# Inverses of the recurrent heads: row steps on blocks of 32 with a block product, or on blocks of 16 with two correction steps on TensorE

## The chip, the cores and the metric

The kernel runs on one core of a Trainium2 chip. The metric is the device time of one execution in microseconds. TensorE (PE in the profile) multiplies matrices and writes to PSUM, VectorE (DVE), ScalarE (ACT) and GpSimd (POOL) do elementwise work, and SyncE (SP) issues most DMA transfers. Each engine runs its own instructions in the order in which they were built, and waits on semaphores for the others.

## The reference, cut to what matters

One layer of a hybrid decoder for a prompt of 256 tokens and 8 single decode tokens: a half-step SwiGLU feed-forward network (FFN), then a mixing stage with 16 attention heads beside 16 recurrent heads (RWKV-7) of size 64, then a second FFN. Everything is float32. The recurrent part of the prompt is this scan:

```python
def step(S, inp):
    r_t, lw_t, k_t, v_t, kk_t, a_t = inp
    sa = jnp.einsum('bhij,bhj->bhi', S, -kk_t)
    S = (S * jnp.exp(lw_t)[:, :, None, :] + sa[..., None] * (kk_t * a_t)[:, :, None, :]
         + v_t[..., None] * k_t[:, :, None, :])
    return S, jnp.einsum('bhij,bhj->bhi', S, r_t)
```

The kernel works on it in chunks of 64 tokens. Inside a chunk the terms `sa` depend on each other through a strictly triangular 64x64 matrix G of products of the scaled kk and b vectors, so each head and chunk needs the inverse of (I - G): 16 heads x 4 chunks = 64 inverses.

## The kernel before, in words

The token columns are T = 264 (256 + 8). `first_ffn` streams weights through `gemm`: a tile of 128x512 float32 is loaded by SP (`raw`, six buffers), split by ACT into a rounded part (`hi`, L122) and by DVE, or POOL for one chunk in four of the mixing stage, into the rest (`lo`, L57), and three products per 128 rows accumulate in a PSUM bank `acc`. `mixing` does the same with the 38 column tiles of w_in (`win`), then w_out in three passes, and `second_ffn` follows.

The work between the weight products is made of Python generators. `spawn` puts one in a list, and `tick`, called after each chunk of four weight blocks in `win` and in w_out, advances each by one `yield`. `pause(n)` skips n ticks. So `yield` and the constants DWAIT, PW and NSTEP decide how the small work is interleaved in the program. A scheduler then reorders instructions within each engine's queue by its own model of time and priorities; what it makes of a program can be read from the built instruction lists.

The pairs of heads p = 0 to 7 are grouped in four batches of n = 2. For each pair `prep` forms decays, normalised keys and the score matrices: `gm` (L423) is the masked 128x512 tile of one half h for four chunks, whose left 64 columns hold G in the rows of the same half. `gm` is stored to DRAM (`scr`, named sa in the profile), L426. When a batch's pairs are done (`bt.left`), `chain` goes on:

- X and Y are loaded from `scr` as one row of partitions for each 32x32 diagonal block, in four copies (ng = 4) that share the columns of the work (L475, L476; tiles X and Xt).
- 30 steps, each a multiplication into `st` and an addition into Y on DVE (L486, L487), invert the 32x32 blocks.
- Y goes to DRAM (`scr2`, named sb, L491) and comes back as `TT` with tokens on partitions (L496). DWAIT ticks are left for each of the two trips.
- The identity is added (L503), the upper left block transposed by DVE (TN, L506), and two rounds of sixteen 32x32 products (L513, L524), each followed by an ACT copy (zs, TT), fill the off-diagonal block.
- TT multiplies KR (`wus`, L538), and products with W, uv and gm, three state steps S, the group norm and the output gate follow.

`dec_rwkv` updates the decode states in 16 slices on DVE and POOL (tiles ld, t, sa, yr), and `attend` handles two heads of attention: scores (L73 m<-s,q), softmax on DVE and ACT, three transposes a head (L730 to L732), and products with V. All of this runs among the w_in products. Before the first pass of w_out, `need` drains what that pass depends on; `drain` ticks all tasks, the other chains and the attention among them. The program's three passes of w_out take pairs 0 to 5, the attention, and pairs 6 and 7.

`early(pi)` issues DMAs on ACT's queue, held in program order, during the first FFN.

Of the kernel before, what the change touches and what calls it, by code (L numbers as in the profile page):

```python
# [7 lines left out]
F32 = mybir.dt.float32  # L8
F32R = mybir.dt.float32r
AF = mybir.ActivationFunctionType  # L10
ALU = mybir.AluOpType
AX = mybir.AxisListType

P = 128
# [10 lines left out]
HALF = (slice(0, 64), slice(64, 128))  # L25
PARTS = [8, 7, 7, 7, 7, 7]
BATCH = [2, 2, 2, 2]
# [2 lines left out]
NS, NH, NT, NLD = 53, 40, 27, 6  # L30
NGM, NKR, NUV, NTT = 10, 5, 3, 2
NSTEP = 4
DWAIT = (8, 8, 8, 4)
LOP = (8,)
PW = (2, 1, 3, 2, 2)
ALPHA = math.exp(-0.5)
# [10 lines left out]
def body(tc, I, O):  # L47
    nc = tc.nc
    V, A, G, TE, SP = nc.vector, nc.scalar, nc.gpsimd, nc.tensor, nc.sync
# [6 lines left out]
    def tt(e, out, a, b, op):  # L56
        return e.tensor_tensor(out=out, in0=a, in1=b, op=op)  # L57

    def stt(out, a, s, b, op0, op1):
        return V.scalar_tensor_tensor(out=out, in0=a, scalar=s, in1=b, op0=op0, op1=op1)  # L60

    def ts(e, out, a, s1, op0, s2=None, op1=None):
        k = {} if op1 is None else dict(op1=op1)
        e.tensor_scalar(out=out, in0=a, scalar1=s1, scalar2=s2, op0=op0, **k)  # L64
# [4 lines left out]
    def bc(ap, shape):  # L69
        return ap.broadcast_to(list(shape))  # L70

    def mm(out, lhsT, rhs, start=True, stop=True, **k):
        TE.matmul(out, lhsT, rhs, start=start, stop=stop, **k)  # L73
# [16 lines left out]
    def pause(n):  # L90
        for _ in range(n):
            yield

    with ExitStack() as ctx:
# [4 lines left out]
        dp = ctx.enter_context(tc.tile_pool(name="dp", bufs=1, space=bass.MemoryType.DRAM))  # L99
# [5 lines left out]
        def tmp(shape=(P, T), dt=F32):  # L105
            pool, n = cur[0]
            return pool.tile(list(shape), dt, tag="t", bufs=n, name=uid("t"))
# [4 lines left out]
        def mp():  # L112
            return pp.tile([P, 512], F32, tag="m", bufs=NM, name=uid("m"))
# [41 lines left out]
        class Norm:  # L155
# [11 lines left out]
            def square(self, x, e=0, pin=False):  # L167
                sq = slot()
                keep = tc.keep_in_program_order if pin else lambda i: i
                if e:  # L170
                    keep(tt(V, sq, x, x, ALU.mult))
                else:
                    keep(act(sq, x, AF.Square))
                self.sums[e].append(sq)
                if len(self.sums[e]) == 3:
                    a, b, c = self.sums[e]
                    keep(tt((G, V)[e], b, b, a, ALU.add))
                    self.sums[e] = [b, c]
# [10 lines left out]
        def early(pi):  # L189
            keep = tc.keep_in_program_order  # L190
            if pi == 1:
                keep(A.dma_start(C, I["cst"]))
                keep(A.dma_start(ss, I["shs"]))
            elif pi in (2, 3):
                nm, ck = (("ks", "ck"), ("vs", "cv"))[pi - 2]
                keep(A.dma_start(O[nm][:, 0:127, :], I[ck][:, 1:128, :]))
# [93 lines left out]
        def mixing_body(mx, n2, n3):  # L290
# [3 lines left out]
            def ring(shape, tag, bufs):  # L294
                return mx.tile(list(shape), F32, tag=tag, bufs=bufs, name=uid(tag))
# [6 lines left out]
            ident, bo, cm = C[:, CID:CID + P], C[:, CBO:CBO + P], C[:, CCM:CCM + P]  # L302
# [12 lines left out]
            sa = fix((P, 64), "sa")  # L315
            yd = fix((P, 64), "yd")
            nbat = len(BATCH)
            scr = [dp.tile([BATCH[b] * 16, 1024], F32, tag=f"sa{b}", name=f"sa{b}") for b in range(nbat)]
            scr2 = [dp.tile([BATCH[b] * 16, 1024], F32, tag=f"sb{b}", name=f"sb{b}") for b in range(nbat)]
            mixed = [None] * 16  # L320
            have = [False]

# [28 lines left out]
            def prep(p, bt, k, xrr, xk, xv):  # L351
# [7 lines left out]
                sg, a = tmp(), tmp()  # L359
# [56 lines left out]
                for h in range(2):  # L416
                    r = HALF[h]
                    gp = mp()
                    for c in range(4):
                        mm(gp[:, c * P:(c + 1) * P], BK[r, c, :, :], KR[r, 0:2, c, :])  # L420
                    gm = ring((P, 4, P), "gm", NGM)
                    bt.Gm[k][h] = gm
                    tt(V, gm, gp.rearrange("p (c t) -> p c t", c=4), bc(msk.unsqueeze(1), (P, 4, P)), ALU.mult)  # L423
                    for blk in range(2):
                        x = blk * 32
                        SP.dma_start(  # L426
                            scr[bt.i].rearrange("(h b k c) (s t) -> h b k s c t", h=2, b=2, c=4, s=32)[h, blk, k],
                            gm[h * 64 + x:h * 64 + x + 32, :, x:x + 32])
                    yield
                kp = mp()  # L430
                for tb in range(2):
# [31 lines left out]
            def chain(bt):  # L463
                n = bt.n
                while bt.left:
                    yield
                nr = n * 16
                ng = P // nr
                if ng == 3:
                    ng = 2  # L470
                nj = 32 // ng
                X = ring((ng * nr, 32, 32), "X", 1)
                Y = ring((ng * nr, nj, 32), "Xt", 1)
                for g in range(ng):
                    SP.dma_start(X[g * nr:(g + 1) * nr], scr[bt.i].rearrange("r (s t) -> r s t", s=32))  # L475
                    SP.dma_start(Y[g * nr:(g + 1) * nr],  # L476
                                 scr[bt.i].rearrange("r (j g t) -> g r j t", g=ng, t=32)[g])
                TT = ring((P, n * 4, 64), "TT", NTT)
                for h in range(2):
                    G.memset(TT[h * 64 + 32:h * 64 + 64, :, 0:32], 0.0)  # L480
                yield from pause(DWAIT[bt.i])
                for s in range(1, 31):
                    m, w = -(-s // ng), 31 - s
                    t = ring((ng * nr, m, w), "st", 2)
                    shp = (ng * nr, m, w)
                    tt(V, t, bc(X[:, s:s + 1, s + 1:], shp), bc(Y[:, :m, s:s + 1], shp), ALU.mult)  # L486
                    tt(V, Y[:, :m, s + 1:], Y[:, :m, s + 1:], t, ALU.add)  # L487
                    if s % NSTEP == 0:
                        yield
                for g in range(ng):  # L490
                    SP.dma_start(scr2[bt.i].rearrange("r (j g t) -> g r j t", g=ng, t=32)[g], Y[g * nr:(g + 1) * nr])  # L491
                yield from pause(1)
                for h in range(2):
                    for blk in range(2):
                        x = h * 64 + blk * 32
                        SP.dma_start(TT[x:x + 32, :, blk * 32:blk * 32 + 32],  # L496
                                     scr2[bt.i].rearrange("(h b m) (s t) -> h b s m t", h=2, b=2, s=32)[h, blk])
                yield from pause(DWAIT[bt.i])
                for h in range(2):
                    for blk in range(2):  # L500
                        x = h * 64 + blk * 32
                        v = TT[x:x + 32, :, blk * 32:blk * 32 + 32]
                        tt(V, v, v, bc(ident[x:x + 32, x:x + 32].unsqueeze(1), (32, n * 4, 32)), ALU.add)  # L503
                TN = ring((P, n * 4, 32), "TN", 1)
                for h in range(2):
                    V.transpose(TN[h * 64:h * 64 + 32], TT[h * 64:h * 64 + 32, :, 0:32])  # L506
                yield
                ps = mp()
                for h in range(2):
                    for k in range(n):  # L510
                        for c in range(4):
                            j = k * 4 + c
                            mm(ps[h * 64 + 32:h * 64 + 64, j * 32:j * 32 + 32],  # L513
                               bt.Gm[k][h][h * 64:h * 64 + 32, c, 32:64], TN[h * 64:h * 64 + 32, j, :])
                zs = ring((P, n * 4, 32), "zs", 1)
                for h in range(2):
                    r = slice(h * 64 + 32, h * 64 + 64)
                    A.copy(zs[r], ps[r, :n * P].rearrange("p (c t) -> p c t", t=32))
                yield
                ps = mp()  # L520
                for h in range(2):
                    r = slice(h * 64 + 32, h * 64 + 64)
                    for j in range(4 * n):
                        mm(ps[h * 64:h * 64 + 32, j * 32:j * 32 + 32], zs[r, j, :], TT[r, j, 32:64])  # L524
                for h in range(2):
                    r = slice(h * 64, h * 64 + 32)
                    A.copy(TT[r, :, 32:64], ps[r, :n * P].rearrange("p (c t) -> p c t", t=32))
                yield
                Ys = [slot() for _ in range(n)]
                uv = bt.UV  # L530
                W, PT = ring((P, n, 3, 64), "W", 1), ring((P, n, 3, 64), "PT", 1)
# [350 lines left out]
        def second_ffn(n3, xr):  # L882
            fin = Norm(VGF)
            with tc.tile_pool(name="f2", bufs=1) as fp:
# [14 lines left out]
                for q in range(4):  # L899
# [6 lines left out]
                            tt(G if j == 2 and q < 3 else V, y[:, j], yg[o], rstd, ALU.mult)  # L906
                    (SP, A)[q % 2].dma_start(O["yT"][:, q * 4:q * 4 + 4, :], y)

        xsp = [dp.tile([P, T], F32, tag=f"xsp{o}", name=f"xsp{o}") for o in range(KD)]
        n2, n3 = Norm(VGM), Norm(VG2)  # L910
        first_ffn(n2)
# [100 lines left out]
```

## Time and profile before

| | us |
|---|---|
| runs, median of 3 (lowest, highest) | 2129.2 (2127.75, 2129.91) |
| the profiled execution, its own time | 2127.34 |
| its span, first to last instruction | 2125.2 |
| PE busy in the span | 2043.9 |
| DVE busy | 1334.3 |
| ACT busy | 1045.8 |
| POOL busy | 419.5 |

The profile is that of one execution. A row of a timeline has the start, the duration, the engine, the source line, the operation, the tiles written and read with their shapes, the number of instructions merged (x) and, in brackets, the engine's idle time before it with what ended it. Rows of groups have the count, the busy time in us and the mean in ns. PE's matmuls are pipelined: a row's duration is longer than its share of PE's time, which is read from start to start. A float32 product leaves two records; the weight products, in a reduced format, leave one. PEclk is the clock granted to TensorE, as a fraction of full speed.

### The profile page before, as it was taken

Reading aid. Unit: us, or ns where it says so; the run is one execution under the profiler, and the core shown is the slowest. Engines: PE = TensorE matmul, PEld = TensorE weight load, DVE = VectorE, ACT = ScalarE, POOL = GpSimd, SP = SyncE. Lnnn points to the kernel's source line nnn. Section 1 sums busy time; section 2 is a strip of 40 time slices with the busy share of each in tenths; the row PEclk is TensorE's granted clock in tenths of the full one; section 3 lists DMA queues with packets and bytes.
Section 4 is the critical chain, followed back from the end, with each engine's and each line's share of the span. In section 5 each row is a group of like instructions: output and inputs, shape, how many; then the busy total and the mean of one; then the engine's idle time right before and its main releaser. Section 6 shows DMA issues by size and latency. Waiting matters only on the chain.

```text
span 2125.2 us, 45168 instructions
## 1 busy us (share of the span) xinstructions
PE 2043.9 (96%) x16870; PEld 1995.4 (94%) x16870; DVE 1334.3 (63%) x2551; ACT 1045.8 (49%) x2002; POOL 419.5 (20%) x581
## 2 busy tenths in 40 slices
PE   8999999999999999989996899999999999999997
PEld 8999999999999999888885679899999999999997
DVE  5765555556555677766888646755555565555555
ACT  5644444444444566546542344644444444444445
POOL 0301011010201146533454201220110102011012
PEclk9999999999999999989997579999999999999999
DMA  6565565656555574434343145456555565555554
GB/s 224 176 182 182 175 205 175 207 180 183 181 177 185 185 227 139 122 96 135 112 136 114 41 138 186 156 182 181 181 175 187 177 184 181 177 186 176 186 176 140
DMA packets 227532, 356.27 MB, mean 168 GB/s; under 512 B 42176, under 2 KB 83152, under 8 KB 227280
## 3 DMA queue, kind: packets, MB, share of 16 engines
q1 hardware_dynamic: 221616, 344.72, 51.8%
q10 hardware_dynamic: 5696, 8.66, 1.1%
q8 instruction: 132, 2.16, 0.4%
q14 instruction: 88, 0.72, 0.1%
HBM read 345.15 MB, written 10.21 MB: 167 GB/s over the span
## 4 chain that ended last, share of the span: by engine, by line
PE 86%; DVE 7%; DMA 2%; ACT 1%; issue 1%; POOL 1%; SPq 1%; DVEq 0%; POOLq 0%; ACTq 0%
PE acc L73 79%; PE m L73 6%; DVE lo L57 1%; DMA raw<-in_gu 1%; DVE Xt L57 1%; DVE st L57 1%; ACT L67 1%; DVE ld L57 0%; ACT t L67 0%; DMA sb<-Xt 0%; DVE s L60 0%; DVE t L57 0%; DMA TT<-sb 0%; DVE TT L57 0%; DVE t L64 0%
## 5 line engine op out<-in xcount | busy, mean ns | idle before, releaser
L73 PE MATMUL acc<-s,hi 128*128 128x264 f32 x7072 | 1317.5, 286 | 10.0 <-ACT hi L122 8.3
L57 DVE TENSOR_TENSOR lo<-raw,hi 128x512 fp32r<-128x512 f32 (+1 forms) x1266 | 861.7, 684 | 600.6 <-ACT hi L122 578.7
L122 ACT CAST hi<-raw 128x512 fp32r<-128x512 f32 (+2 forms) x1304 | 780.5, 602 | 909.5 <-PE acc L73 830.6
L73 PEld LDWEIGHTS acc<-s,hi 128*128 128x128 f32 x7072 | 1108.8, 190 | 17.8 <-ACT hi L122 8.5
L73 PE MATMUL acc<-s,lo 128*128 128x264 f32 x3536 | 1016.1, 288 | 12.7 <-DVE lo L57 10.5
L73 PEld LDWEIGHTS acc<-s,lo 128*128 128x128 f32 x3536 | 669.9, 189 | 18.5 <-DVE lo L57 14.1
L73 PE MATMUL acc<-t,hi 128*128 128x264 f32 x2752 | 502.7, 284 | 1.6 <-ACT t L251 1.6
L73 PEld LDWEIGHTS acc<-t,hi 128*128 128x128 f32 x2752 | 426.0, 188 | 1.9 <-ACT t L251 1.8
L57 POOL TENSOR_TENSOR t<-t,t 128x264 f32<-128x264 f32 (+1 forms) x162 | 173.0, 1068 | 1209.6 <-ACT hi L122 897.6
L73 PE MATMUL acc<-t,lo 128*128 128x264 f32 x1376 | 388.2, 284 | 0.0
L73 PEld LDWEIGHTS acc<-t,lo 128*128 128x128 f32 x1376 | 258.2, 188 | 0.0
L57 DVE TENSOR_TENSOR t<-acc,t 128x264 f32<-128x264 f32 x164 | 70.9, 433 | 36.7 <-PE acc L73 36.5
L57 POOL TENSOR_TENSOR s<-s,s 128x264 f32<-128x264 f32 (+1 forms) x56 | 49.5, 886 | 195.8 <-ACT s L67 179.1
L57 POOL TENSOR_TENSOR lo<-raw,hi 128x512 fp32r<-128x512 f32 x38 | 49.7, 1308 | 57.4 <-ACT hi L122 57.2
L67 ACT ACT_TABLE_LOAD x42 | 53.9, 1283 | 1.9 <-PEq L1004 1.2
L60 DVE SCALAR_TENSOR_TENSOR s<-acc,s 128x264 f32<-128x264 f32 x96 | 40.7, 428 | 16.8 <-PE acc L73 16.3
L60 DVE SCALAR_TENSOR_TENSOR x<-acc,x 128x264 f32<-128x264 f32 x96 | 40.6, 427 | 10.9 <-PE acc L73 10.4
L57 DVE TENSOR_TENSOR st<-X,Xt 128x60 f32<-128x60 f32 (+10 forms) x120 | 36.1, 300 | 10.1 <-DMA Xt<-sa 7.4
L67 ACT ACTIVATE t<-t 128x264 f32<-128x264 f32 x94 | 40.0, 425 | 3.3 <-DVE t L57 1.8
L57 DVE TENSOR_TENSOR Xt<-Xt,st 128x60 f32<-128x60 f32 (+10 forms) x120 | 36.7, 305 | 1.7
L251 ACT CAST t<-t 128x264 fp32r<-128x264 f32 x86 | 35.5, 413 | 3.6 <-POOL t L57 2.1
L73 PE MATMUL m<-s,hi 128*128 128x264 f32 x160 | 30.1, 287 | 0.4 <-ACT hi L122 0.4
(209 smaller groups left out, 1116.5 us busy)
## 6 DMA issues: line engine op xcount, KB each, us to landing
raw<-in_gu SPq DMA_DIRECT2D x688, 256.0 KB, 3.2
raw<-in_dn SPq DMA_DIRECT2D x224, 256.0 KB, 2.7
raw<-in_win SPq DMA_DIRECT2D x152, 256.0 KB, 3.2
raw<-in_dn SPq DMA_DIRECT2D x160, 192.0 KB, 2.7
raw<-in_wout SPq DMA_DIRECT2D x48, 256.0 KB, 3.0
raw<-in_wout SPq DMA_DIRECT2D x32, 128.0 KB, 2.4
xsp<-x ACTq DMA_DIRECT2D x16, 132.0 KB, 3.5
s<-xsp SPq DMA_DIRECT2D x16, 132.0 KB, 3.0
```

Of the source, the lines that this page charges most:

```text
L57: return e.tensor_tensor(out=out, in0=a, in1=b, op=op)
L60: return V.scalar_tensor_tensor(out=out, in0=a, scalar=s, in1=b, op0=op0, op1=op1)
L67: return A.activation(out=out, in_=in_, func=f, **k)
L73: TE.matmul(out, lhsT, rhs, start=start, stop=stop, **k)
L122: A.copy(hi[:, :w], raw[:, :w])
L251: A.copy(hi, u)
```

## The change

The inverse of each 64x64 matrix is started from four 16x16 diagonal blocks instead of two 32x32 blocks, and finished by two correction steps with full 64x64 products.

- `gm` is stored whole, 64x64, one DMA for each half and pair instead of two. The rows of `scr` are 4 x 1040 long, so that the four diagonal blocks of 16 lie at a constant stride (`diag`).
- X is loaded by one DMA, 64 partitions of 16x16, and no second copy Y. POOL writes ones on the diagonal. 14 steps of two DVE instructions invert the blocks in place.
- X goes to the diagonal blocks of `scr2`, whose other entries were set to zero by eight DMAs from ACT's queue in the first FFN. U is read back in two DMAs. DVE transposes U into W (tile Wt) in blocks of 32.
- Twice: times(low, W) multiplies with G, F = 2I - W + that product, and U becomes U times F, with W recomputed the first time. That makes five rounds of sixteen 64x64 products. The result takes the place of TT.
- DWAIT becomes (4, 4) for all batches, the pauses after the load of X and after that of U.

```diff
-DWAIT = (8, 8, 8, 4)
+DWAIT = (4, 4)
...
+                z = tmp((P, 260))
+                G.memset(z, 0.0)
+                for d in scr2:
+                    for x in d.rearrange("(q r) x -> q (r x)", q=2):
+                        keep(A.dma_start(x.rearrange("(p x) -> p x", p=P), z))
...
-                    for blk in range(2):
-                        x = blk * 32
-                        SP.dma_start(
-                            scr[bt.i].rearrange("(h b k c) (s t) -> h b k s c t", h=2, b=2, c=4, s=32)[h, blk, k],
-                            gm[h * 64 + x:h * 64 + x + 32, :, x:x + 32])
+                    w = (h * bt.n + k) * 4
+                    SP.dma_start(scr[bt.i][w:w + 4, 0:4096].rearrange("c (s t) -> s c t", s=64), gm[r, :, 0:64])
...
-                for s in range(1, 31):
-                    m, w = -(-s // ng), 31 - s
...
+                nr, nj = n * 32, n * 4
+                X = ring((nr, 16, 16), "X", 2)
+                def diag(x):
+                    return (x.rearrange("r (b x) -> (r b) x", b=4)[:, 0:1024]
+                            .rearrange("r (s u) -> r s u", u=64)[:, :, 0:16])
+                SP.dma_start(X, diag(scr[bt.i]))
+                yield from pause(DWAIT[0])
+                G.memset(X.rearrange("r s t -> r (s t)")[:, 0:256:17], 1.0)
+                for s in range(1, 15):
+                    w = 15 - s
+                    t = ring((nr, s, w), "st", 2)
+                    tt(V, t, bc(X[:, s:s + 1, s + 1:], (nr, s, w)), bc(X[:, :s, s:s + 1], (nr, s, w)), ALU.mult)
+                    tt(V, X[:, :s, s + 1:], X[:, :s, s + 1:], t, ALU.add)
                     if s % NSTEP == 0:
                         yield
...
+                SP.dma_start(diag(scr2[bt.i]), X)
                 yield from pause(1)
...
+                U, W = square("U"), square("Wt", 1)
                 for h in range(2):
+                    SP.dma_start(U[HALF[h]], scr2[bt.i][h * nj:(h + 1) * nj, 0:4096].rearrange("j (s t) -> s j t", s=64))
+                yield from pause(DWAIT[1])
+                V.transpose(W, U)
+                def times(a, b):
+                    ps = mp()
                     for k in range(n):
+                        for h in range(2):
+                            r = HALF[h]
+                            for c in range(4):
+                                j = k * 4 + c
+                                mm(ps[r, j * 64:j * 64 + 64], a(k, h, c), b[r, j])
+                    return ps[:, :nj * 64].rearrange("p (j t) -> p j t", t=64)
+                def part(x):
+                    return lambda k, h, c: x[HALF[h], k * 4 + c]
+                def low(k, h, c):
+                    return bt.Gm[k][h][HALF[h], c, 0:64]
+                for last in (False, True):
+                    ps = times(low, W)
+                    F = square("F", 1)
+                    stt(F, W, -1.0, bc(I2.unsqueeze(1), (P, nj, 64)), ALU.mult, ALU.add)
+                    tt(V, F, ps, F, ALU.add)
+                    yield
+                    pu = times(part(F), U)
+                    if not last:
+                        pw = times(part(U), F)
+                        W = square("Wt", 1)
+                        A.copy(W, pw)
+                    U = square("U")
+                    V.tensor_copy(U, pu) if last else A.copy(U, pu)
+                    yield
+                TT = U
```

More of the change, by code (lines that the diff above doesn't have):

```diff
@@ L317, in mixing_body @@
             nbat = len(BATCH)
-            scr = [dp.tile([BATCH[b] * 16, 1024], F32, tag=f"sa{b}", name=f"sa{b}") for b in range(nbat)]
-            scr2 = [dp.tile([BATCH[b] * 16, 1024], F32, tag=f"sb{b}", name=f"sb{b}") for b in range(nbat)]
+            scr = [dp.tile([BATCH[b] * 8, GS], F32, tag=f"sa{b}", name=f"sa{b}") for b in range(nbat)]
+            I2 = fix((P, 64), "I2")
+            for h in range(2):
+                ts(G, I2[HALF[h]], ident[HALF[h], HALF[h]], 2.0, ALU.mult)
             mixed = [None] * 16
@@ L466, in chain @@
                     yield
[L467 to L477, printed above, removed]
@@ L488, in chain, with square @@
                     if s % NSTEP == 0:
                         yield
-                for g in range(ng):
-                    SP.dma_start(scr2[bt.i].rearrange("r (j g t) -> g r j t", g=ng, t=32)[g], Y[g * nr:(g + 1) * nr])
+                SP.dma_start(diag(scr2[bt.i]), X)
                 yield from pause(1)
+                def square(name, bufs=None):
+                    return ring((P, nj, 64), name, bufs or NTT)
+                U, W = square("U"), square("Wt", 1)
                 for h in range(2):
[L494 to L506, printed above, removed]
@@ L519, in chain @@
[L519 to L528, printed above, removed]
+                    SP.dma_start(U[HALF[h]], scr2[bt.i][h * nj:(h + 1) * nj, 0:4096].rearrange("j (s t) -> s j t", s=64))
@@ new lines, in chain @@
+                yield from pause(DWAIT[1])
+                V.transpose(W, U)
+                def times(a, b):
+                    ps = mp()
+                    for k in range(n):
+                        for h in range(2):
+                            r = HALF[h]
[3 more added lines that the diff above has]
+                    return ps[:, :nj * 64].rearrange("p (j t) -> p j t", t=64)
@@ L907, in second_ffn @@
                     (SP, A)[q % 2].dma_start(O["yT"][:, q * 4:q * 4 + 4, :], y)
+        GS = 4 * 1040
+        scr2 = [dp.tile([n * 8, GS], F32, tag=f"sb{b}", name=f"sb{b}") for b, n in enumerate(BATCH)]
         xsp = [dp.tile([P, T], F32, tag=f"xsp{o}", name=f"xsp{o}") for o in range(KD)]
```

19 lines of the change are left out of this document (removed).

## The prediction

> **What bounds the kernel now.** I read the page first, then the busy time in stretches around the recurrent part, then the instruction timelines at the edges of these stretches.
>
> ```profile
> span 2125.2 us, 45168 instructions
> PE 2043.9 (96%) x16870; PEld 1995.4 (94%) x16870; DVE 1334.3 (63%) x2551; ACT 1045.8 (49%) x2002; POOL 419.5 (20%) x581
> ...
> PEclk9999999999999999989997579999999999999999
> ```
>
> TensorE (PE) is busy for 96% of the span at full clock nearly everywhere; the two slices at 7 and 5 tenths lie at 1115 to 1220 us. Only there can an inverse that is off the weight stream matter much. Three stretches follow (span, busy time of PE, weight loads, DVE, ACT and POOL, granted clock, DMA):
>
> ```profile
> 780.00:1067.40 287.40, 268.19 (x2360) 252.04 (x2359) 212.99 (x457) 158.98 (x326) 141.89 (x260) 0.95 0.45 126
> 1067.40:1159.70 92.30, 70.58 (x688) 64.22 (x688) 80.48 (x215) 33.58 (x81) 44.91 (x57) 0.91 0.46 131
> 1159.70:1244.10 84.40, 70.96 (x436) 51.83 (x436) 53.19 (x186) 34.55 (x110) 18.36 (x34) 0.60 0.20 60
> ```
>
> Their edges, from the timelines of DVE and PE:
>
> ```profile
> 1066.07 1.29 DVE L57 TENSOR_TENSOR gm<-m,C 128x512 f32<-128x512 f32 x2 [1.12 <-PE m L73]
> 1146.95 0.29 PE L73 MATMUL acc<-s,lo 128*128 128x264 f32 x1
> 1158.07 0.41 DVE L57 TENSOR_TENSOR TT<-TT,C 32x256 f32<-32x256 f32 x1 [6.17 <-DMA TT<-sb]
> 1159.68 1.03 PE L73 MATMUL m<-TN,gm 32*32 32x32 f32 x16 [12.44 <-DVE TN L506]
> 1244.12 0.81 PE L73 MATMUL acc<-s,hi 128*128 128x264 f32 x2
> ```
>
> Stretch one ends with the last score matrix (gm) of the fourth batch. PE is the bound there: 268.2 of 287.4 us, 19.2 idle. Stretch two is bound by DVE: 80.5 of 92.3 us, while PE has no weights left at 1147 and waits 12.4 us for the inverse. Stretch three, the tail up to the first w_out product, has no weight products in before: PE runs the last chain and the attention heads at a clock of 0.60, which is why it looks 71.0 us busy. I call them stage, middle and tail.
>
> **The change part by part.** Four prices first: weight products; a run of eight 64x64 products (each f32 product leaves two records, so x16 is eight); a batch's sixteen 32x32 products; and state steps and the rest of a chain.
>
> ```profile
> 1277.24 61.84 PE acc L73 x505
> ...
> 995.52 0.96 PE L73 MATMUL m<-uv,gm 64*64 64x64 f32 x16
> ...
> 999.86 1.09 PE L73 MATMUL m<-TN,gm 32*32 32x32 f32 x32
> ...
> 1024.18 0.45 PE L73 MATMUL m<-S,PT 64*64 64x64 f32 x8
> 1024.46 0.40 PE L73 MATMUL m<-kr,S 64*64 64x64 f32 x8
> 1024.79 0.51 PE L73 MATMUL acc<-s,hi 128*128 128x264 f32 x2
> ...
> 1031.38 1.03 PE L73 MATMUL m<-s,C 128*128 128x256 f32 x4
> 1169.46 3.67 PE L73 MATMUL m<-kr,TT 64*64 64x128 f32 x16 [0.45 <-ACT TT L527]
> ...
> 1179.60 0.47 PE L73 MATMUL m<-t,W 64*64 64x64 f32 x2
> ...
> 1187.99 0.45 PE L73 MATMUL m<-N,PT 64*64 64x64 f32 x8
> ```
>
> A weight product costs 61.84/505 = 0.1225 us. A correction step makes products of sixteen 64x64 pieces, four in a row on one half: 2 x 0.96 = 1.92 us at full clock. A batch has five of them, 9.6 us, where it had two rounds of 1.09, 2.2 us: 7.4 us more TensorE work per batch, 29.6 in all.
>
> *Stage.* The built order of the changed program puts each chain nearer to its own scores, and so the fourth batch's scores later: 225 weight products still stand between them and w_out, where 342 did. What comes ahead of the mark: 117 x 0.1225 = 14.3 us of weights; the third batch's chain behind its inverse, in before after the mark: 2 x 3.67 halved for the clock 3.7, the products from 1179.60 to 1187.99 halved 4.2, three state steps of 0.61 (1024.18 to 1024.79) 1.8, and 1.0 for s,C: 10.7; the new products of three batches less the old ones of two, 28.8 - 4.4 = 24.4. Together 49.4 us of PE work on a stretch where PE is the bound. DVE loses work there (below), and part of the 19.2 us in which PE stood idle waiting for DVE goes. Bounds: none of it, or all. I take 8, since each batch still has two trips through DRAM with DVE's in-order queue behind them. Stage: **+41**, from +30 to +49.
>
> *Middle.* The row steps go from 60 to 28 DVE instructions a batch, the four additions of the identity and two transposes give way to one transpose, two F steps of two instructions and one copy.
>
> ```profile
> L57 DVE TENSOR_TENSOR st<-X,Xt 128x60 f32<-128x60 f32 (+10 forms) x120 | 36.1, 300 | 10.1 <-DMA Xt<-sa 7.4
> ...
> L57 DVE TENSOR_TENSOR Xt<-Xt,st 128x60 f32<-128x60 f32 (+10 forms) x120 | 36.7, 305 | 1.7
> ...
> L57 DVE TENSOR_TENSOR TT<-TT,C 32x256 f32<-32x256 f32 x16 | 9.3, 582 | 12.1 <-DMA TT<-sb 11.8
> L506 DVE STREAM_TRANSPOSE TN<-TT 32x256 f32<-32x256 f32 x8 | 3.5, 432 | 0.2
> L57 DVE TENSOR_TENSOR gm<-m,C 128x512 f32<-128x512 f32 x16 | 10.6, 680 | 1.2 <-PE m L73 1.1
> ```
>
> Steps: 32 fewer x 0.30 = 9.7 us a batch. TT and TN were 12.8/4 = 3.2; the new ones are six passes over 128x512 elements, by gm's 0.68 about 4.1. DVE gains some 9 us a batch. In the new order, 109 DVE instructions lie between the fourth batch's scores and its transposed U, where 217 did: the heads, weight splits and third chain that stood among them are elsewhere. At the middle's 80.48/215 = 0.374 us each that is 41 us of work for 80.5. Beside it DVE was idle for 92.3 - 80.5 = 11.8 us, 6.2 of it the wait for TT. The DRAM trips, with KB and microseconds to landing:
>
> ```profile
> X<-sa SPq DMA_DIRECT2D x16, 128.0 KB, 3.4
> ...
> sa<-gm SPq DMA_DIRECT2D x32, 16.0 KB, 2.1
> Xt<-sa SPq DMA_DIRECT2D x16, 32.0 KB, 3.0
> sb<-Xt SPq DMA_DIRECT2D x16, 32.0 KB, 2.7
> TT<-sb SPq DMA_DIRECT2D x16, 32.0 KB, 2.0
> ```
>
> SP's 96 issues of these become 32, but X waits on SP for the scores to land (2.1 + 3.0 us, with 1 for two issues) while only one weight split is ready on DVE: 5.5 us idle. The second trip, 2.7 + 2.0 + 1.5 for three issues, has 18 DVE instructions in front of the transpose: 1 us. The raw weights queued behind X on SP are six tiles ahead. With the other 5.6 us of idle as before: 41 + 12 = 53 us instead of 92. Middle: **-39**, from -45 (waits all covered) to -30 (an instruction mix as heavy as 0.45 each). PE has 177 x 0.1225 = 21.7 us of weights there, so it isn't the bound, and it stalls at the first product as it does now.
>
> *Tail.* The new order has 16 heads behind the first product, where 14 were. Ten heads in before:
>
> ```profile
> 1200.74 0.42 PE L730 MATMUL m<-C,t 128*128 128x128 f32 x1
> ...
> 1238.96 0.48 PE L730 MATMUL m<-C,t 128*128 128x128 f32 x1 [2.91 <-DVE t L64]
> ```
>
> Nine intervals of 38.2 us, 4.25 each: two more are 8.5. The last 48 weight products move in too, 5.9 us or 9.8 at the 0.60 clock; they stand in the chain's gaps (PE idles 13.4 us of the tail), so I take 3, bounds 0 and 9.8. The products: 7.4 us more, 12.3 at that clock; DVE and ACT steps between them leave PE to the heads, so I take 8.5, bounds 3 and 12.3. Tail: **+20**, from +8 to +31.
>
> *Edits with one answer.* The eight zero fills go out on ACT in the first FFN; like the two loads there, they fall between casts that wait for PE anyway:
>
> ```profile
> 148.72 0.94 ACTq L193 DMA_DIRECT2D ss<-in_shs  x1
> 149.80 0.62 ACT L122 CAST hi<-raw 128x512 fp32r<-128x512 f32 x1 [0.84 <-PE acc L73]
> ```
>
> Two issues of some 0.4 us fit each gap of 0.84: nothing; without that cover, 3 us. The memsets on POOL (idle 80%) and ACT's two copies for four cost nothing either.
>
> Sum: +41 - 39 + 20 = +22 us on the profiled execution's 2127.3 (its span and 2.1 around it); the runs' median is 1.9 above that, so 2129.2 + 22 = **2151 us**.
>
> **Rivals.**
> *The clock comes back (faster).* The tail's PE work is 71.0 x 0.60 = 42.6 us at full clock; with 7.4 of products, 5.9 of weights and 2 x 2.55 of heads it is 61, and with 13.4 of idle 74: -10 instead of +20, so -8 in all, 2121; with the stage's idle gone too, 2110. It decides once the tail's granted clock is above some 0.85. For it: there is more to fill gaps with. Against it: heads wait for softmax as now, and one wait of 4 us costs the clock:
>
> ```profile
> 1136.17 0.47 PE L730 MATMUL m<-C,t 128*128 128x128 f32 x1 [4.01 <-DVE t L64]
> ...
> 1142.58 0.29 PE L73 MATMUL acc<-s,lo 128*128 128x264 f32 x1
> ```
>
> Here it took 6 us of work until the weight products ran in 0.29 again. [...]
>
> *The halves overlap.* The state steps, whose neighbours lie on different halves of the array, take 0.61/8 = 0.076 us a product against 0.12 for uv,gm. If the corrections ran so, a product of sixteen is 1.2: 10.5 us less in the stage, 3 in the tail, +9, 2138. Against it: the loop runs c innermost, four in a row on one half, as uv,gm does. [...]
>
> *Hidden anyway.* DVE's relief removes all 19.2 us of idle in the stage, and the tail grows by 12: 30 - 39 + 12 = +3, 2132. Against it: PE's waits there came from DVE's order, not its load (213 of 287 us).
>
> *The trip is late.* Its pieces are 64 bytes where they were 128, and the first three batches leave it four pauses instead of eight. If each batch waits 5 us more, +20, 2171. [...]
>
> **How the numbers follow.** Forecast 0.42, clock 0.18, overlap 0.15, hidden 0.13, late trip 0.12. A measurement can't tell less than 0.2% (4.3 us) from no change. Slower: 0.42 + 0.12 and most of overlap, 0.66; same: hidden and the rest of overlap, 0.15; faster: the clock, 0.19. The forecast's own range is +8 to +36, 2137 to 2165; with the clock's nearer end and the late trip, 2122 to 2172.
>
> **What would show it.** Right: the fourth batch's scores at 1095 to 1115 us (now 1067), the first correction product some 53 us behind them, a tail of 95 to 110 us, products of 1.9 us at full clock. Wrong: scores before 1085 (the stage's idle went), a tail under 85 us with a clock above 0.85, or products near 1.2 us. A DVE wait for U over 4 us shows the late trip.

## The result, and the profile after

The changed kernel is slower: 2138.7 us (median of 7 runs, 2135.2 to 2142.1) against 2129.3 (7 runs on the same chip), ratio 1.0041, 95% interval 1.0029 to 1.0053. A second series gave 2143.3 against 2128.3, ratio 1.0061 (1.0041 to 1.0082). The forecast was slower, by 22 us; it is slower by 9 to 15. The size was wrong, and so was one term of the sum.

The page of the changed kernel, first lines and clock:

```profile
span 2137.0 us, 45726 instructions
...
PE 2055.9 (96%) x17254; PEld 2009.2 (94%) x17254; DVE 1309.4 (61%) x2423; ACT 1041.2 (49%) x1992; POOL 432.4 (20%) x580
...
PEclk9999999999999999999997779999999999999999
...
L73 PE MATMUL m<-Wt,gm 64*64 64x64 f32 x256 | 14.2, 247 | 25.8 <-DVE Wt L498 25.8
```

DVE lost 25 us of work and 128 instructions; PE gained 12 us and 384 records. The cold slices read 7, 7, 7 where they read 7, 5, 7; the prediction names the first two of these and not the third, at 1222 to 1275 us. The last row is new: PE waits 25.8 us for the transposed U, 20.2 of them before the fourth batch's first product (below).

The three stretches of the prediction, and then the w_out passes and the second FFN (span, busy PE, weight loads, DVE, ACT, POOL, granted clock, DMA share, GB/s), changed kernel:

```profile
780.00:1105.70 325.70, 312.40 (x3047) 293.29 (x3046) 211.53 (x395) 170.26 (x343) 153.14 (x267) 0.97 0.42 119
1105.70:1158.30 52.60, 29.48 (x242) 27.55 (x241) 47.64 (x111) 18.31 (x43) 37.46 (x41) 0.80 0.45 128
1158.30:1250.10 91.80, 75.10 (x597) 56.95 (x597) 66.13 (x229) 37.46 (x124) 28.17 (x47) 0.74 0.26 77
...
1250.07:1362.89 112.82, 110.50 (x901) 106.11 (x899) 70.70 (x148) 54.20 (x120) 14.31 (x26) 0.95 0.51 160
1362.89:2136.99 774.10, 759.48 (x6201) 757.85 (x6200) 446.97 (x754) 373.02 (x666) 98.11 (x96) 0.99 0.56 177
```

The last two of the kernel before:

```profile
1244.12:1354.29 110.17, 107.69 (x894) 103.94 (x893) 70.65 (x148) 55.35 (x121) 13.91 (x23) 0.97 0.52 163
1354.29:2125.23 770.94, 756.34 (x6201) 754.70 (x6200) 447.05 (x754) 373.78 (x666) 98.17 (x96) 0.99 0.55 178
```

Their edges, from the changed kernel's timelines of DVE and PE:

```profile
1105.04 0.69 DVE L57 TENSOR_TENSOR gm<-m,C 128x512 f32<-128x512 f32 x1 [0.61 <-PE m L73]
1158.27 2.54 PE L73 MATMUL m<-Wt,gm 64*64 64x64 f32 x32 [20.24 <-DVE Wt L498]
1250.07 0.81 PE L73 MATMUL acc<-s,hi 128*128 128x264 f32 x2
```

The reading that helps most splits PE's time of each stretch into three: its work at full speed (busy time, each instant times the granted clock), its idle time, and what the clock takes (busy time times one less the clock). I worked this out from the matmul and clock records, in steps of 10 ns.

| us | before: span | work | idle | clock | after: span | work | idle | clock |
|---|---|---|---|---|---|---|---|---|
| up to w_in's first result (pj) | 778.2 | 768.3 | 9.9 | 0.0 | 781.0 | 768.2 | 11.0 | 1.7 |
| stage | 289.2 | 257.1 | 19.0 | 13.0 | 324.7 | 303.1 | 13.1 | 8.5 |
| middle | 92.3 | 67.7 | 21.6 | 3.0 | 52.5 | 27.7 | 23.1 | 1.7 |
| tail | 84.4 | 41.6 | 13.4 | 29.5 | 91.8 | 54.7 | 16.6 | 20.5 |
| w_out passes | 110.2 | 104.1 | 2.4 | 3.7 | 112.8 | 105.3 | 2.2 | 5.3 |
| second FFN | 770.9 | 756.4 | 14.6 | 0.0 | 774.1 | 759.5 | 14.6 | 0.0 |
| all | 2125.2 | 1995.2 | 80.9 | 49.2 | 2137.0 | 2018.5 | 80.6 | 37.7 |

So PE has 23 us more to do: twenty correction rounds at 1.47 us (below) less the eight old rounds at 1.03 (start to start too, 999.86 to 1000.89 us in the timeline of before) are 21.2, and 3.1 come in the second FFN. Its idle time is the same, and the clock gives 11.5 back. The middle's 40 us are not a saving: its work went to the stage and the tail, and the wait for the inverse stayed. DVE's relief bought no idle time of PE. Why not is what the experiments answer.

### The profile page after: what moved, and what is told of

Its sections match the earlier page's. It is cut to its first block, busy times and chain, and to the rows that moved or that the text cites. A ratio compares the mean times of both kernels' runs of the same rounds, so it can differ in the third digit from the quotient of the medians.

```text
span 2137.0 us, 45726 instructions
## 1 busy us (share of the span) xinstructions
PE 2055.9 (96%) x17254; PEld 2009.2 (94%) x17254; DVE 1309.4 (61%) x2423; ACT 1041.2 (49%) x1992; POOL 432.4 (20%) x580
## 4 chain that ended last, share of the span: by engine, by line
PE 88%; DVE 6%; DMA 2%; issue 1%; ACT 1%; POOL 1%; SPq 0%; DVEq 0%; ACTq 0%; POOLq 0%
PE acc L73 80%; PE m L73 8%; DVE lo L57 1%; DVE X L57 1%; DVE st L57 1%; DMA raw<-in_gu 1%; DVE ld L57 0%; ACT L67 0%; DMA U<-sb 0%; DVE t L64 0%; DVE t L57 0%; DMA sb<-X 0%; DVE s L60 0%; ACT t L67 0%; DMA raw<-in_win 0%
## 5 line engine op out<-in xcount | busy, mean ns | idle before, releaser
L73 PE MATMUL acc<-s,hi 128*128 128x264 f32 x7072 | 1318.6, 287 | 11.5 <-ACT hi L122 9.9
L57 DVE TENSOR_TENSOR t<-acc,t 128x264 f32<-128x264 f32 x164 | 70.9, 433 | 37.7 <-PE acc L73 37.5
L73 PE MATMUL m<-Wt,gm 64*64 64x64 f32 x256 | 14.2, 247 | 25.8 <-DVE Wt L498 25.8
L73 PEld LDWEIGHTS m<-Wt,gm 64*64 64x64 f32 x256 | 13.1, 154 | 27.1 <-issue 26.5
L256 ACT CAST t<-t 128x264 fp32r<-128x264 f32 x86 | 35.5, 413 | 3.7 <-POOL t L57 2.1
```

What stands on the lines that cost most here:

```text
L256: A.copy(hi, u)
```

## The experiments

These runs were taken on four chips, each beside the kernel before on its own chip, whose medians were 2127.6 to 2128.7 us.

**The changed kernel again** (a2).

> The changed kernel once more, unedited. Its first profile lost 2.8 us ahead of w_in (first pj at 781.0 us, before 778.2), 2.6 in the w_out passes and 3.2 in the second FFN (756.5 us, before 753.3), where the change puts no work but the zero fills. If these belong to the change, the same three numbers come again within 1 us and the ratio to before is 1.004 again. If they are the spread of executions, each moves by 2 us or more, some of them below the number of before.

Measured: 2143.3 us, 1.0061. First pj at 779.5, w_out 113.1 us, second FFN 774.1. So the loss ahead of w_in is the spread of executions: over all thirteen profiles it lies between 777.9 and 781.8, whether the program fills zeros or not. The other two repeat and belong to the program (see the end).

**The zero fills alone** (b_zero), added to the kernel before:

```diff
+                z = tmp((P, 260))
+                G.memset(z, 0.0)
+                for d in scrz:
+                    for x in d.rearrange("(q r) x -> q (r x)", q=2):
+                        keep(A.dma_start(x.rearrange("(p x) -> p x", p=P), z))
```

> The kernel before with the eight zero fills of the change alone, at the same place on ACT's queue in the first FFN, into buffers that nothing reads. Theory (hidden): first pj at 778.2 +-1 us and a ratio of 1.000 +-0.0007. Rival (the 2.8 us that the changed kernel lost ahead of w_in are the fills): first pj at 781, ratio 1.0013.

Measured: 2127.9 us, ratio 1.0001 (0.9991 to 1.0011). The time says hidden, as predicted; first pj stood at 781.8 in the profiled execution all the same, so that one mark can't price 3 us.

**Each correction product twice** (a_dbl):

```diff
-                                mm(ps[r, j * 64:j * 64 + 64], a(k, h, c), b[r, j])
+                                for _ in range(2):
+                                    mm(ps[r, j * 64:j * 64 + 64], a(k, h, c), b[r, j])
```

> Each 64x64 product of the correction steps is issued twice in a row into the same place, so 20 rounds of sixteen products more; the instruction order is otherwise that of the changed kernel. Theory (a round costs what the trace shows start to start, 1.44 us at full clock, and is paid where it stands): stage 3 x 5 x 1.44 = 21.6 less a part of the 13.3 us of idle, +12 to +21; middle +0; tail 7.2 at the clock of 0.74 = +9.7; together +22 to +31 over the changed kernel. Rival 1 (a round costs the 1.92 us of the prediction): +38 at full clock, over +40 with the tail. Rival 2 (the rounds stand in gaps in which PE waits for DVE anyway): under +12. Rival 3 (more work in the tail brings its clock back): the tail grows by less than 4 us and its granted clock rises over 0.80.

Measured: 2183.8 us, 1.0260 (1.0244 to 1.0276), 40 us over the changed kernel beside it; stage 361.0, middle 52.5, tail 111.0. The theory's 22 to 31 us were passed. Rival 1 came near in time (over 40) and in the price of an added round, 1.87 us, but not in that of a round as it stands, 1.47. Rivals 2 and 3 failed: the added work was not hidden, and it lost more clock instead of winning it back. The round's price, start to start, from PE's timelines of the changed kernel and of this one:

```profile
896.45 1.54 PE L73 MATMUL m<-Wt,gm 64*64 64x64 f32 x32
897.92 0.71 PE L73 MATMUL m<-t,C 128*128 128x264 f32 x2
```

```profile
906.00 3.40 PE L73 MATMUL m<-Wt,gm 64*64 64x64 f32 x64
909.34 0.49 PE L73 MATMUL m<-t,C 128*128 128x264 f32 x1
```

One round takes 897.92 - 896.45 = 1.47 us, not the 1.92 of the prediction; a doubled one 3.34, so 1.87 more for sixteen products that follow their twin into the same place. The split of its profiled execution, the slowest of the five, gives work +35.0, idle -3.8 and clock +22.0 against the first profile of the changed kernel. In the tail the clock fell from 0.74 to 0.65: more work there doesn't by itself bring it back.

**Halves alternating in the rounds** (a_alt):

```diff
-                        for h in range(2):
-                            r = HALF[h]
-                            for c in range(4):
+                        for c in range(4):
+                            for h in range(2):
+                                r = HALF[h]
```

> The sixteen products of a round in another order: neighbours lie on different halves of the partitions (c outside, h inside), as in the state steps, instead of four in a row on one half; nothing else moves. Theory (neighbours on different halves run at the state steps' 0.076 us a product): 1.2 us a round instead of 1.44, 20 rounds, -4.8 at full clock, stage -3 to -4, tail -1 to -2, whole -3 to -5 against the changed kernel. Rival (0.09 is already what these products take, whatever their order): a round stays at 1.4 to 1.5 us and the time within 1.5 us.

Measured: 2132.4 us, 1.0017 (1.0005 to 1.0030), 11 us less than the changed kernel beside it. Its timeline of PE:

```profile
898.52 1.15 PE L73 MATMUL m<-Wt,gm 64*64 64x64 f32 x32
899.60 0.71 PE L73 MATMUL m<-t,C 128*128 128x264 f32 x2
```

A round is 1.08 us, 0.068 a product, where four in a row on one half took 1.47, 0.092 a product: -0.39, and 20 rounds give 7.8, which is what the split shows (work 2011.7 us against 2019.9 in a2). The rest of the gain lies within what executions of the changed kernel differ by (2130 to 2147 in that series).

**The old inverse with the new pauses** (b_w4):

```diff
-DWAIT = (8, 8, 8, 4)
+DWAIT = (4, 4, 4, 4)
```

> The kernel before with pauses of 4 ticks for each trip (DWAIT = 4, 4, 4, 4), nothing else: the order of the change without its inverse. In the built order the fourth batch's scores have 144 weight products left behind them, where 342 were. Theory (the earlier order only moves TensorE's work ahead of the scores, and the inverse on DVE, 60 instructions a batch, still sets the middle): the stage grows by 198 x 0.1225 = 24 us and a chain's 11, the middle stays at 70 us or more with only 18 us of weights in it, so PE's idle there grows from 22 to 45 us or more; the whole 2140 to 2160. Rival (the order alone shortened the middle, whatever the inverse): middle at 50 to 55 us and the whole within 6 us of 2128.

Measured: 2185.4 us, 1.0272 (1.0257 to 1.0287): 58 us lost by the pauses alone, where the theory had 12 to 32. Its three stretches and PE's wait for the inverse, from the windows and the page:

```profile
780.00:1139.70 359.70, 325.79 (x2809) 305.75 (x2807) 234.02 (x490) 169.67 (x348) 153.05 (x270) 0.91 0.43 116
1139.70:1219.30 79.60, 37.59 (x258) 32.80 (x256) 67.26 (x186) 20.71 (x57) 39.61 (x50) 0.69 0.34 92
1219.30:1301.00 81.70, 73.56 (x440) 53.94 (x440) 51.61 (x186) 31.85 (x108) 16.55 (x31) 0.59 0.22 61
```

```profile
L73 PE MATMUL m<-TN,gm 32*32 32x32 f32 x128 | 7.2, 218 | 34.2 <-DVE TN L506 34.2
```

The middle shortens to 79.6 and half of it is PE's idle time (42.0 us); the stage pays 70. PE's work hardly changes (2000.4 us); idle goes from 80.9 to 111.3 and the clock's part from 49.2 to 71.7.

**The new inverse with pauses of 8** (a_w8):

```diff
-DWAIT = (4, 4)
+DWAIT = (8, 8)
```

> The changed kernel with the old pauses (DWAIT = 8, 8), nothing else. In the built order 318 weight products stand behind the fourth batch's scores, where 225 did, and the first correction product waits behind 313 of them and 12 head transposes, where 177 and none stood. Theory (TensorE's work is the same wherever it stands, and the time is that work, PE's idle and the clock's loss): stage -11 to -20 us, the middle fuller and PE's idle in it down from 24 to under 10, the tail within 8 us; whole -5 to -15 against the changed kernel. Rival (the longer pauses put the last chain later, and the tail grows by what the middle gains): whole within 4 us of the changed kernel or above it.

Measured: 2123.4 us, 0.9984 (0.9975 to 0.9993), 15 to 20 below the changed kernel's two medians and 4 below the kernel before. I call these the old pauses, but the kernel before has 8, 8, 8 and 4: its fourth batch waits only half as long, and no run gave the new inverse just that.

```profile
780.00:1068.10 288.10, 279.52 (x2678) 262.40 (x2677) 202.32 (x362) 159.76 (x325) 149.83 (x263) 0.99 0.46 126
1068.10:1161.90 93.80, 75.34 (x676) 67.55 (x674) 80.66 (x188) 31.84 (x82) 48.31 (x58) 0.87 0.41 112
1161.90:1239.50 77.60, 61.21 (x524) 46.13 (x523) 52.01 (x180) 33.13 (x104) 18.36 (x34) 0.71 0.24 70
```

The stage is as long as that of the kernel before (289.2 us), with 279.0 us of work in it where that had 257.1: the rounds were paid by idle time (19.0 to 8.4) and by the clock (13.0 to 1.7). The theory had the direction and not the sizes: the stage fell by 35.6 us where it said 11 to 20, the tail by 14.2 where it said at most 8, and PE's idle time in the middle only to 18.5 where it said under 10. The wait that stood in the changed kernel's page is gone, but PE's idle time as a whole fell only from 80.6 to 70.1 us: in place of the 25.8 it waits more for the softmax of the heads (12.6 us where 8.8) and for a state step (7.9). From the groups of PE and DVE between 780 and 1260 us, this kernel:

```profile
L73 PE MATMUL m<-Wt,gm 64*64 64x64 f32 x256 | 12.8, 225 | 0.0
...
L60 DVE SCALAR_TENSOR_TENSOR F<-Wt,I 128x512 f32<-128x512 f32 x8 | 5.9, 742 | 6.0 <-ACT Wt L526 5.9
L498 DVE STREAM_TRANSPOSE Wt<-U 128x512 f32<-128x512 f32 x4 | 2.8, 712 | 17.3 <-DMA U<-sb 17.3
```

and the changed kernel:

```profile
L60 DVE SCALAR_TENSOR_TENSOR F<-Wt,I 128x512 f32<-128x512 f32 x8 | 5.5, 693 | 22.7 <-ACT Wt L526 22.7
L498 DVE STREAM_TRANSPOSE Wt<-U 128x512 f32<-128x512 f32 x4 | 2.8, 708 | 11.4 <-DMA U<-sb 11.4
```

DVE waits longer for U with the old pauses, and PE, which has weights to run, does not wait for the transposed U at all; DVE waits less for ACT's copy, which waits for PE's rounds.

**The row steps' multiplications twice**, with the pauses of 4 (a_st2) and of 8 (a_w8st2):

```diff
-                    tt(V, t, bc(X[:, s:s + 1, s + 1:], (nr, s, w)), bc(X[:, :s, s:s + 1], (nr, s, w)), ALU.mult)
+                    for _ in range(2):
+                        tt(V, t, bc(X[:, s:s + 1, s + 1:], (nr, s, w)), bc(X[:, :s, s:s + 1], (nr, s, w)), ALU.mult)
```

> The changed kernel with each of the 14 multiplications of the row steps issued twice into the same place: 14 DVE instructions of about 0.2 us a batch more, no work on TensorE. In the built order the fourth batch's scores have 192 weight products behind them instead of 225. Theory (the middle is DVE's, the stage PE's): middle 118 instructions instead of 109, +2 to +5 us, with PE's idle in it up by as much and 4 more; stage + 33 x 0.1225 = 4; whole +4 to +10 over the changed kernel. Rival (DVE has room in both): within 2 us of the changed kernel.

> The changed kernel with the old pauses (8, 8) and the 14 multiplications of the row steps issued twice: the same 18 us of DVE work more as in the run with the pauses of 4, which cost 22 us there. Theory (what the short pauses lack is cover: with more weight products between the loads, the steps and the first correction round, the inverse's time on DVE stays behind TensorE's work): +0 to +8 us over the run with the old pauses alone (2123), so 2123 to 2131, and PE's wait for Wt under 8 us. Rival (each microsecond of the row steps reaches the end whatever the pauses): +18 to +22, 2141 to 2146.

Measured: 2161.4 us, 1.0160 (1.0143 to 1.0177), with the pauses of 4; 2113.2, 0.9927 (0.9913 to 0.9940), with those of 8. The multiplications on DVE, in the changed kernel, a_st2, a_w8 and a_w8st2:

```profile
L57 DVE TENSOR_TENSOR st<-X 64x14 f32<-64x14 f32 (+6 forms) x56 | 20.8, 372 | 10.2 <-DMA X<-sa 9.7
L57 DVE TENSOR_TENSOR st<-X 64x14 f32<-64x14 f32 (+6 forms) x112 | 39.0, 349 | 11.2 <-DMA X<-sa 9.8
L57 DVE TENSOR_TENSOR st<-X 64x14 f32<-64x14 f32 (+6 forms) x56 | 15.0, 268 | 16.2 <-DMA X<-sa 15.0
L57 DVE TENSOR_TENSOR st<-X 64x14 f32<-64x14 f32 (+6 forms) x112 | 29.2, 261 | 13.9 <-DMA X<-sa 11.5
```

With short pauses 18 us of DVE work cost some 20, more than the theory's 4 to 10: in the profiled execution, the slowest of the four, 16 us more idle on PE and 12 more of the clock. With long pauses the same edit added 14 us to DVE, not the 18 that was expected, since each multiplication is shorter there (see the end). It cost nothing, and that kernel is even 10 us faster than without it, below the theory's 2123 to 2131. The order moved a little with the edit (the fourth batch's scores stand 19 weight products later), DVE's wait for U went from 17.3 to 3.1 us and PE's idle from 70.1 to 61.9. So a change of order without any purpose is worth about 10 us here, and smaller differences between two orders say nothing about the edit. The change's own loss, 9 to 15 us, is about of that size. The row that shows the cover gone, from the page of a_st2:

```profile
L73 PE MATMUL m<-Wt,gm 64*64 64x64 f32 x256 | 14.3, 247 | 35.5 <-DVE Wt L499 35.1
```

**Alternating in all half-array products**: in the rounds, uv,gm, kr,U, t,W and gm,W, uv,t and gm,uv (a_all), the same and its two rounds of 32x32 in the kernel before (b_all), and with the old pauses as well (a_all8). One of the five loops:

```diff
-                    for h in range(2):
-                        r = HALF[h]
-                        for c in range(4):
+                    for c in range(4):
+                        for h in range(2):
+                            r = HALF[h]
                             mm(wus[k][r, c * P:c * P + P], TT[r, k * 4 + c, :], bt.KR[k][r, 0:3:2, c, :])
```

> The changed kernel with halves alternating in the correction rounds and in the chain's and scores' other half-array products too (uv,gm; kr,U; t,W and gm,W; uv,t; gm,uv): loops turned, no work changed. Theory (neighbours on different halves overlap there too, 0.07 us a product instead of 0.10 to 0.12): 4 to 10 us less than with the correction rounds alone, 2122 to 2130, not above the kernel before. Rival (those loops overlap already or wait for DVE): within 2 us of the run with the correction rounds alone, 2130 to 2134.

> The kernel before with halves alternating in the same products, and in its two rounds of 32x32. Theory (the loop order is worth the same without the change): 3 to 8 us below the kernel before, ratio 0.996 to 0.9985, so the change itself still costs about 5 us with both alternated. Rival (before had nothing to overlap): ratio 1.000 +-0.001.

> The changed kernel with both edits: the old pauses (8, 8) and halves alternating in all the half-array products. Theory (the two gains are of different kinds, order and TensorE work, and add): the run with the pauses alone, 2123.4, less the 8 us of TensorE work that the alternated correction rounds save and up to 10 that the other loops gave the kernel before: 2106 to 2116; beside the kernel before with the same loops, 2111, the change is then worth nothing or a gain of a few us. Rival (the gains overlap, since PE has idle time and the clock falls where its work gets shorter): 2117 to 2124, and the change costs some 8 us against the kernel before with the same loops.

Measured: a_all 2130.9 us, 1.0017 (1.0006 to 1.0027), no better than a_alt, so its rival held: 8 us less work on PE than in a_alt, and 9 us more idle. (Their profiled executions also differ by 12 us in the clock; they are the fastest of a_all and the slowest of a_alt.) b_all 2111.1, 0.9929 (0.9914 to 0.9945), far more than forecast: its profiled execution, the fastest of six, has 9 us less work and 10 more idle than the kernel before, and the clock takes 21 less. a_all8 2108.9, 0.9909 (0.9894 to 0.9924): inside its theory's range and faster than both kernels of this study. Against b_all the difference is 0.0020 of 2128 us, 4 us, give or take as much: with the same loops and the old pauses (but for the fourth batch's) the change is a small gain or none, as in a_w8. The stretches of a_all8:

```profile
780.00:1065.30 285.30, 274.81 (x2732) 257.69 (x2731) 204.85 (x369) 162.16 (x329) 146.62 (x265) 0.99 0.46 132
1065.30:1153.60 88.30, 68.85 (x638) 61.87 (x636) 76.75 (x186) 29.41 (x74) 46.44 (x56) 0.85 0.36 105
1153.60:1224.10 70.50, 50.15 (x516) 36.52 (x515) 49.46 (x178) 33.55 (x106) 15.56 (x30) 0.78 0.26 77
```

## Why the prediction was right or wrong

*Stage, +41 forecast, +35.5 measured: within its range.* The work is +46.0 us where the sum had 49.4. A round is 1.47 us and not 1.92, so the new products of three batches are 22 and not 28.8; that makes 42.6, and the other 3.4 are not accounted for. The 0.96 us of uv,gm was the duration of its row; start to start (995.52 to 996.42) it was 0.90, and the rounds ran faster still. Idle time gave back 5.9, and the clock, which the sum left at full here, 4.5, where 8 was taken. The rival "hidden anyway" had all idle go; 13.1 of 19.0 stayed.

*Middle, -39 forecast, -39.8 measured: right in kind, and in size by luck.* DVE sets it, but its instructions were heavier (47.6/111 = 0.43 us instead of 0.374, 47.6 us of work instead of 41) and its idle smaller (5.0 instead of 12), and the two errors cancel. In the whole program DVE lost 25 us, some 6 a batch, where 9 were forecast.

*Tail, +20 forecast, +7.4 measured: the step that failed.* Its terms were two heads 8.5, weights 3, products 8.5 (with the lower bounds 0 and 3 they make 11.5, not the +8 of its range). The tail in two parts, from the first product to the third head's transposes and from there to w_out, kernel before and changed kernel:

```profile
1159.70:1188.60 28.90, 28.00 (x246) 23.76 (x246) 16.35 (x47) 6.20 (x21) 8.53 (x12) 0.53 0.11 33
1188.60:1244.10 55.50, 42.96 (x194) 28.08 (x190) 36.84 (x140) 28.35 (x89) 9.83 (x22) 0.64 0.25 73
```

```profile
1158.30:1185.80 27.50, 24.57 (x353) 22.52 (x353) 20.05 (x53) 6.50 (x21) 9.78 (x14) 0.88 0.20 63
1185.80:1250.10 64.30, 50.53 (x246) 34.43 (x244) 46.08 (x176) 30.96 (x103) 18.39 (x33) 0.68 0.28 83
```

The second part has 14 heads instead of 12, with 21 of the weights and one state step more, and is 8.8 us longer; the heads' 8.5 fit, if the rest fell into gaps. The first part holds the rounds and the other 27 weights and is 1.4 us shorter, where products and weights were to add 11.5 to the tail. Its work at full speed rose from 14.9 to 21.6 us and its idle time from 0.9 to 2.9, but the clock took 3.0 where it had taken 13.0: before, the half clock lasted 27 us into the tail, now 7. I had priced the new work at the old clock of 0.60, as if the clock were a property of the place. The rival "the clock comes back" named this term. Its tail clock, 0.74, stayed under the 0.85 at which it was to decide: the heads behind the chain ran at 0.64 before and at 0.68 after. That the clock made the difference is read from these rows and from two runs. In a_dbl the half clock lasted 40 us into the tail, and this part took 49 us with 7 us more work. In a_alt it lasted 19, and the part took 29.0 us, 1.5 longer than in the changed kernel: the clock took 6.0 more, with 2.3 less work and 2.1 less idle time. So the sign agrees, but part of what the clock takes is idle time otherwise, and no run set the clock by itself. Kernels with 12, 14 and 16 heads behind the first product (a_w8, before, changed) have tails of 77.6, 84.4 and 91.8 us, 3.4 to 3.7 a head, as if rounds and weights cost nothing there.

*Overlap, a rival at 1.2 us a round:* in the order as written, four in a row on one half, a round took 1.47, between it and the forecast's 1.92. In a_alt, where neighbours lie on different halves, it took 1.08; that this rival's 2138 is the time measured is luck. *The late trip:* DVE waited 11.4 us for U in all, once 5.4, which is over the sign's 4. But before the fourth batch, where PE waits 20.2 us, DVE did not wait for U: its row steps and the decode state's slices keep it busy until the transpose.

```profile
1157.43 0.70 DVE L498 STREAM_TRANSPOSE Wt<-U 128x512 f32<-128x512 f32 x1
```

In a_w8 DVE waits 17.3 us for U, and PE does not wait behind it. The trip is not the cause. *Zero fills:* nothing, as said.

*Not foreseen:* +2.6 us in w_out, where the clock takes 1.6 more and the work is 1.2 longer, and +3.2 in the second FFN. Together with the marks before w_in they hide that stage, middle and tail sum to +3.1 us in the profiled execution, where +22 was forecast; that the measured time still lies in the forecast's range is luck.

*What the prediction saw and blamed too little:* the cost came with the pauses more than with the rounds. It saw that the order moved the scores, priced that as work put ahead of a mark, and did not ask what the same inverse would do under the old pauses. There the rounds vanish in PE's idle time and in the clock. Short pauses cost 58 us with the old inverse, in three batches, and 15 to 20 with the new one, in four: that fits DVE's relief, which the changed kernel spent on an order that leaves PE to wait 25.8 us for the transposed U. How much of the 15 to 20 us is these waits, and how much is the clock or an order that happens to be worse, is open.

## What to carry to other kernels

Where one engine is busy 96% of the time, add up its work, its idle time and what the clock takes, each for the whole program; a stretch that gets 40 us shorter because its work moved has saved nothing. When a change brings new constants for the interleaving along with a new algorithm, try the algorithm under the old ones first, and expect the order alone to move the time: one edit that was meant to do nothing for speed moved it by 10 us here. Try products on half the array in loops whose neighbours lie on different halves: here a round of sixteen took 1.08 us that way and 1.47 us with four in a row on one half.

## What the runs showed of the hardware

*The clock.* In every profile the half-clock stretches begin and end on one grid of 3.41 us; in the kernel before those inside the span last 3.41, 6.83, 13.65, 34.13 or 37.55 us. Counted over the thirteen profiles, window by window: of 92 windows at full clock in which PE was busy less than half the time, 78 were followed by a window at half clock; of 102 busy between 0.5 and 0.7, 24; of 7433 busier ones, 14. Out of half clock: of 119 windows busy under 0.8 none was followed by full clock, of 234 that were busy throughout 106. (The ends of products are modelled, so a few windows may belong to the neighbouring class.) So a wait need not fill a window. In a_alt one of 2.44 us was enough; 2.3 of it lie in one window. PE's timeline:

```profile
881.31 0.28 PE L73 MATMUL acc<-s,lo 128*128 128x264 f32 x1
884.04 1.97 PE L73 MATMUL m<-Wt,gm 64*64 64x64 f32 x32 [2.44 <-DVE Wt L498]
885.94 1.22 PE L73 MATMUL m<-ld,tw 65*128 65x128 f32 x4
```

The round behind it takes 1.90 us instead of 1.08. The same wait in the changed kernel was 2.08 us, lay 1.8 and 0.3 us in two windows, and cost no clock. Where the grid falls on the waits is then a candidate for why executions of one program differ by up to 17 us; that was not tried.

*The second FFN.* It took 770.9 to 771.4 us in three programs (before, b_zero, b_all), 773.1 in three (a_w8, a_all8, a_w8st2) and 774.0 to 774.1 in the other seven, the old inverse of b_w4 among them, with the same 6201 records. Aligned product by product, the difference grows in the gate and up products, by 0.7 ns each on average, and not at all in the down products. In the built programs of the kernel before and the changed one, several of the 32 tiles that hold its inputs lie in other slots of SBUF. Whether that is the cause was not tried; it is not the inverse.

*VectorE beside GpSimd.* The changed kernel's 112 row steps took 41.4 us of DVE and the same 112 in a_w8 31.0. By the instruction records, those that ran while POOL was idle took 185 ns on average (29 of them) and 194 in a_w8 (65); those that ran wholly beside POOL's work took 430 (51, beside it for at least 98% of their time) and 449 (27). In the changed kernel the first kind took up to 209 ns each, the second 164 to 1265, and the 13 that lay inside a single POOL instruction 184 on average. So the order also set what a row step costs, which the forecast took as fixed. POOL's spans are rough, and no run changed POOL's work alone.
